# One more chunk of each FFN by seven products, its downs held back, and three smaller rearrangements

## The chip, the cores and the metric

The kernel runs on one core of a Trainium2 chip. The metric is device microseconds from launch to end. TensorE (PE) multiplies, VectorE (DVE), ScalarE (ACT) and GpSimd (POOL) do everything elementwise, and SyncE (SP) issues most transfers. Six instruction streams run beside each other and wait for one another by semaphores.

## The reference

Two layers work on 512 latent tokens and 256 context tokens of width 1024. Each layer is half an FFN, a token mixer, and half an FFN again; each of these is modulated and closed by a layer norm:

```
u = h * (1 + scale) + shift                     # from a conditioning vector: c @ w_mod
y = (silu(u @ w_in_a) * (u @ w_in_v)) @ w_out   # FFN: 1024 -> 2 x 2816 -> 1024
h = LN(ALPHA * h + 0.5 * gate * y) * g + b
```

Mixer 0 is neighbourhood attention on a 8 x 64 grid, mixer 1 grouped-query attention in a window of 128 tokens with a sink logit; both also read all context keys. In layer 1, the context is not needed after the mixer's keys and values, so the last FFN (1b) works on the 512 latent tokens alone. All is in float32.

## The kernel before, in words

Activations lie transposed: `z[d]` (128 channels x 768 tokens, d = 0 to 7) is the residual, `uh[d]` and `ul[d]` are the high and low part of the modulated input u. Every product runs as three matmuls (high x high, high x low, low x high; `mm3`, L155 to L157), so every weight is split too: `wunit` loads a unit of 128 x 2048 in four quarters (`wr`), and `split_w` makes the high part by an ACT cast (L102) and the low part by a subtraction on POOL or DVE (L104). With `mem` given, the low part is made otherwise: ACT writes the negated source (L108), and a transfer issued by POOL adds the weight to it from memory (L109, an "adding transfer"). The pairs go through a ring of 8 buffers (`RING`), the raw quarters through 5.

The four FFNs are 0a, 0b (layer 0), 1a, 1b (layer 1), all made by `ffn`. Its 2816 hidden channels are worked off in 11 chunks of 256 (`NCH`). A chunk has three units: two for a and v (`av`; `pa`, `pv`), and one for the downs (`down`; `pd`), which add gate x product to `z` (`accumulate`, L473) and so need the gate. Tokens come in two groups: a is the 512 latent and b the 256 context tokens in 0a, 0b and 1a; in 1b they are the two halves of the latent.

- Chunks 0 and 1 run plainly. In chunk 1 `sums` and `fourth` prepare combinations of u's quarters, and `fourth` overwrites half of `uh`, `ul` for d = 0 to 3; `save` has put that half to memory.
- Chunks 2 to 8 take a and v by seven products in place of eight (`seven`, after Winograd): `quarters` loads a unit's four quarters and makes seven pairs from them, three of them plain quarters (a11, a12, a22), four sums (s1 to s4). Their downs follow one unit late (`lagging`), with weights by adding transfers.
- `restore` brings the saved half back under chunk 8's downs.
- Chunks 9 and 10 run plainly: chunk 9 for group a, chunk 10 for a and then b, and chunk 9 for b with its weights loaded again (`r`).

In between lie the background products of DVE (`gemv_dve`, L202), which make later modulation vectors row by row; `tick` deals them out at a set pace. In 0a the first 33 steps (32 products) make the gate itself (`late_gate`).

A layer norm comes in parts: `sums` over d, `mean` (a matmul, L424), `centers` and squares, `variance` (L447), reciprocal root and `spreading` (L377), then `out`, which makes the next u (L305 to L310). The parts are put at named places (`plan`, `at`): the name of a down, a query tile or an attention block. `post(0)` of an FFN's end calls those of group a, `post(1)` the first of group b.

The kernel's text is a priority, not the order of an engine's queue: the framework plans each queue by a simulated time and takes what is ready. `behind(x, y)` fixes an order of two instructions of one engine. Memory comes in phases: pool "S" has 12 slabs (used for down weights, temporaries and the mixers' tiles), pool "T" the sums of u; `t2` is a set of six buffers for everybody.

Of the kernel before, what the change touches and what calls it, by code (L numbers as in the profile page):

```python
# [13 lines left out]
ALU = mybir.AluOpType  # L14
# [24 lines left out]
def hybrid_kernel(ctx: ExitStack, tc: tile.TileContext, h0, cc, crow, wmod, wmodt, bmod, lnp, wst,  # L39
# [73 lines left out]
    def phase(x):  # L113

        if phase_of[0] != x:
            phase_of[1].close()
            ph.clear()
            phase_of[0] = x
            ph[x] = phase_of[1].enter_context(tc.tile_pool(name=f"ph{x}", bufs=1, reuse_waits="tile"))

    def wunit(slabs=False, again=None, adding=False):
# [4 lines left out]
        for q in range(4):  # L126
# [3 lines left out]
            if slabs:  # L130
                hi, lo = [ph["S"].tile([P, 512], F32R, tag="slab", name=f"w{x}{nm}", bufs=SLABS) for x in "hl"]
            else:
                hi, lo = ring_pair(nm)
# [13 lines left out]
    last_pe, agenda = [None], {}  # L147
# [5 lines left out]

    def mm3(ps, a, b, first, last):
        nc.tensor.matmul(ps, a[0], b[0], start=first, stop=False)  # L155
# [131 lines left out]
    def mod_out(nm, d, c0, c1, st, prm, rm=False, dd=None):  # L287
# [12 lines left out]
        else:  # L300
            uf = ph["S"].tile([P, 512], F32, tag="slab", name=f"uf{nm}_{d}", bufs=SLABS)
# [107 lines left out]
    def layer_norm(nm, c0, c1, tag, pool=False):  # L409
# [16 lines left out]
        def centers():  # L426
            zs = [center(d, c0, c1, v["pm"]) for d in range(DT)]
# [16 lines left out]
        def variance():  # L444
            pv = bank(tag, f"pv{nm}")
            for j in range(nj):
                x = nc.tensor.matmul(pv[:, j:j + 1], v["acc"][:, j * P:(j + 1) * P], onesd[:, 0:1], start=True, stop=True)  # L447
                behind(x, prev_ln[0])
                behind(x, last_pe[0])
            ve = pv[:, 8:8 + nj]  # L450
# [3 lines left out]
        def spreading():  # L454
            v["pr"], prev_ln[0] = spread(nm, v["y"], n, tag)

# [20 lines left out]
    def ffn(nm, groups, gt, mid, post, units=(), opened={}, head=None, apart=None):  # L477

# [69 lines left out]
        def sums(j):  # L548

            x1, x2 = [bank("s", f"x{nm}_{j}_{i}")[:, 0:n2] if paced else t2(f"x{nm}_{j}_{i}")[:, 0:n2] for i in range(2)]  # L550
            x3 = t2(f"x{nm}_{j}_2")[:, 0:n2]
            k = j + 4
            op(nc.vector, x1, (uh[j], 1), (uh[j], 0), ALU.subtract)
            op(nc.vector, x1, x1, (ul[j], 1), ALU.add)
            op(nc.vector, x1, x1, (ul[j], 0), ALU.subtract)
# [3 lines left out]
            op(nc.vector, x2, (uh[k], 1), x1, ALU.subtract)  # L559
            op(nc.vector, x2, x2, (ul[k], 1), ALU.add)  # L560
# [8 lines left out]
        def fourth():  # L569

            for j in range(4):
# [5 lines left out]
                behind(nc.vector.tensor_tensor(out=x, in0=x, in1=y, op=ALU.add), evacuated[0])  # L577
# [8 lines left out]
        def quarters(u):  # L586

            src = wst[u].rearrange("p (k c) -> p k c", c=256)
            a11, a12, a21, a22 = [raw_quarter(src[:, h * 4:h * 4 + 4, m * P:m * P + P], f"{u}_{m}{h}")
                                  for m in range(2) for h in range(2)]  # L590
# [6 lines left out]
            def pair(n, src):  # L597
# [5 lines left out]
            out = [pair("a11", a11), pair("a12", a12)]  # L603
# [5 lines left out]
            return out + [pair("s4", s4), pair("s3", s3), pair("a22", a22)]  # L609
# [50 lines left out]
        late_downs, js = [], []  # L660
# [3 lines left out]
        for ci in list(range(NCH)) + [("r", NCH - 2)]:  # L664
            r = isinstance(ci, tuple)
            if not r and 0 < ci < NCH - 2:
                phase("T")
                pace[0] = each * weight[ci] / (4 if ci < s0 else 14)
                if ci == s0 - 1:
                    saved = dp.tile([2, 4, P, n2], F32, name=f"sv{nm}")  # L670
                    save(saved)
                    js = list(range(4))
                    for _ in range(1 if paced else 4):
                        sums(js.pop(0))
            if not r and s0 <= ci < NCH - 2:
# [759 lines left out]
```

## Time and profile before

| what | number |
|---|---|
| median of 3 runs (lowest to highest) | 2791.89 us (2791.28 to 2796.59) |
| the profiled execution: its time, its span | 2795.03 us, 2793.3 us |
| mean granted TensorE clock | 0.983 |
| busy: PE, DVE, POOL, ACT | 2686.0, 1819.2, 1690.1, 1214.7 us |
| matmuls | 17050 |
| read from memory, written | 312.98 MB, 12.25 MB |

The stages begin, by the trace, at about: 0a 0 us, mixer 0 575 us, 0b 1005 us, 1a 1545 us, mixer 1 2076 us, 1b 2384 us. PE's busy time has matmuls overlapping, so a busy share near one says that PE has work, not how fast it goes; the distance from one matmul to the next says that. "Busy" of a named line, its mean length and what ended the idle time before it are read from the groups of instructions; who waits for whom, from the table of waits.

### The profile page before, as it was taken

To read this page: it belongs to the slowest core of one execution; us is meant where nothing else is said; L and a number is where in the kernel's file an instruction comes from. 1 tells how busy PE (TensorE), PEld (TensorE's weight loads), DVE (VectorE), ACT (ScalarE), POOL (GpSimd) and SP (SyncE) were. 2 spreads that over 40 slices of the span, in tenths; PEclk is the share of its full clock that TensorE was granted. 3 is DMA by queue.
4 is the path that set the end of the run, shared out by engine and by line. 5 is a ranking of instruction groups with operands and counts; after the bars stand their busy time and mean duration, and the time that the engine had idled before them with its cause. 6 is when DMAs were issued, how large, how long until landed. Compare 5 with 4: busy or idle time off the path is not lost.

```text
span 2793.3 us, 48152 instructions
## 1 busy us (share of the span) xinstructions
PE 2686.0 (96%) x17050; PEld 2425.9 (87%) x17050; DVE 1819.2 (65%) x4190; ACT 1214.7 (43%) x2493; POOL 1690.1 (61%) x1528
## 2 busy tenths in 40 slices
PE   8799999999999989999999999999998999889997
PEld 5699999888888888999988899999886777889997
DVE  4977776565555686666645676666466667777744
ACT  4234343366345343443433434344246544444543
POOL 4487664474434565867644777766466446677763
PEclk9899999999999999999999999999999999999998
DMA  8465656332221213454553336467532111235562
GB/s 315 139 175 160 167 155 183 96 101 71 57 57 53 66 46 91 121 139 130 139 140 88 95 89 168 129 193 199 155 89 57 31 31 46 69 89 129 134 174 68
DMA packets 289952, 324.00 MB, mean 116 GB/s; under 512 B 28592, under 2 KB 178224, under 8 KB 288688
## 3 DMA queue, kind: packets, MB, share of 16 engines
q1 hardware_dynamic: 273296, 291.42, 35.0%
q0 software_dynamic: 16128, 29.37, 6.3%
q8 instruction: 135, 2.21, 0.3%
q14 instruction: 105, 0.86, 0.1%
q10 hardware_dynamic: 288, 0.14, 0.0%
HBM read 312.98 MB, written 12.25 MB: 116 GB/s over the span
## 4 chain that ended last, share of the span: by engine, by line
PE 80%; DVE 9%; ACT 2%; issue 2%; DMA 2%; POOL 1%; POOLq 0%; DVEq 0%; ACTq 0%; SPq 0%
PE pd0b L155 2%; PE pd1a L155 2%; PE pd0b L156 2%; PE pd0b L157 2%; PE pd1a L156 2%; PE pd1a L157 2%; PE pd0a L155 2%; PE pd0a L156 2%; PE pd0a L157 2%; DMA wr<-in_wst_dram 1%; PE wo L828 1%; PE o L828 1%; PE pd1b L155 1%; DVE z L473 1%; PE pd1b L157 1%
## 5 line engine op out<-in xcount | busy, mean ns | idle before, releaser
L104 POOL TENSOR_TENSOR wl<-wr,wh 128x512 fp32r<-128x512 f32 x296 | 389.2, 1330 | 259.8 <-ACT wh L102 192.9
L104 POOL TENSOR_TENSOR wl_s<-S,wh_s 128x512 fp32r<-128x512 f32 x210 | 279.2, 1368 | 43.3 <-ACT wh_s L102 43.1
L102 ACT CAST wh_s<-S 128x512 fp32r<-128x512 f32 x224 | 135.8, 620 | 357.0 <-POOL S L594 111.5
L102 ACT CAST wh<-wr 128x512 fp32r<-128x512 f32 x296 | 178.8, 619 | 205.1 <-DMA wr<-in_wst_dram 55.4
L202 DVE CUSTOM_DVE_ANT_0 jk<-wt,cb 128x512 f32<-128x512 f32 x364 | 247.5, 680 | 25.5 <-DMA wt<-in_wmodt_dram 21.9
L594 POOL TENSOR_TENSOR S<-wr,wr 128x512 f32<-128x512 f32 x112 | 152.9, 1365 | 157.9 <-DMA wr<-in_wst_dram 138.8
L104 POOL TENSOR_TENSOR wl_a<-wr,wh_a 128x512 fp32r<-128x512 f32 x126 | 167.6, 1383 | 14.1 <-ACT wh_a L102 11.4
L102 ACT CAST wh_a<-wr 128x512 fp32r<-128x512 f32 x168 | 103.9, 621 | 137.1 <-PE pd1b L156 19.2
L473 DVE SCALAR_TENSOR_TENSOR z<-pd0b,gt,z 128x256 f32<-128x256 f32 (+1 forms) x176 | 103.2, 602 | 57.1 <-PE pd0b L157 56.9
L473 DVE SCALAR_TENSOR_TENSOR z<-pd1a,gt,z 128x512 f32<-128x512 f32 (+1 forms) x168 | 100.0, 619 | 45.8 <-PE pd1a L157 45.3
L473 DVE SCALAR_TENSOR_TENSOR z<-pd0a,gt,z 128x512 f32<-128x512 f32 (+1 forms) x168 | 99.7, 620 | 31.3 <-PE pd0a L157 31.1
L835 POOL TENSOR_SCALAR p<-p,l 128x512 f32<-128x512 f32 x64 | 44.5, 697 | 120.8 <-DVE l L941 115.3
L323 POOL TENSOR_SCALAR z<-z,ag_None,ab_None 128x256 f32<-128x256 f32 (+1 forms) x78 | 63.2, 816 | 47.7 <-DVE uh L309 36.4
L835 POOL TENSOR_SCALAR pw<-pw,l 128x512 f32<-128x512 f32 (+1 forms) x64 | 41.2, 644 | 69.4 <-DVE l L1132 26.7
L594 POOL TENSOR_TENSOR S<-S,wr 128x512 f32<-128x512 f32 x56 | 79.9, 1428 | 4.0 <-DVE ul L579 1.4
L594 POOL TENSOR_TENSOR S<-wr,S 128x512 f32<-128x512 f32 x56 | 79.2, 1415 | 3.2 <-POOL S L594 0.4
L940 ACT ACTIVATE p<-s,m 128x512 f32<-128x512 f32 x64 | 44.0, 689 | 78.9 <-DVE m L938 73.7
L305 ACT ACTIVATE ufl<-z,bi_None,sc_None 128x256 f32<-128x256 f32 (+1 forms) x86 | 54.6, 654 | 27.4 <-DVE z L458 27.3
L473 DVE SCALAR_TENSOR_TENSOR z<-pd1b,gt,z 128x512 f32<-128x512 f32 (+1 forms) x98 | 56.6, 609 | 14.8 <-PE pd1b L157 14.5
L310 DVE TENSOR_TENSOR ul<-ufl,uh 128x256 fp32r<-128x256 f32 (+1 forms) x88 | 59.9, 686 | 3.0 <-ACT uh L307 1.6
L202 DVE CUSTOM_DVE_ANT_0 jk<-zspare,cb 128x512 f32<-128x512 f32 x84 | 57.1, 679 | 5.1 <-DMA zspare<-in_wmodt_dram 4.5
L155 PE MATMUL vn<-wh,uh 128*128 128x256 f32 x192 | 54.8, 286 | 0.9 <-DVE nq L782 0.6
(1467 smaller groups left out, 10613.5 us busy)
## 6 DMA issues: line engine op xcount, KB each, us to landing
wr<-in_wst_dram SPq DMA_DIRECT2D x520, 256.0 KB, 3.4
wt<-in_wmodt_dram SPq DMA_DIRECT2D x208, 256.0 KB, 3.9
zspare<-in_wmodt_dram SPq DMA_DIRECT2D x48, 256.0 KB, 4.4
wr_0b<-in_wst_dram SPq DMA_DIRECT2D x43, 256.0 KB, 3.2
wr_1b<-in_wst_dram SPq DMA_DIRECT2D x43, 256.0 KB, 3.2
wr_2b<-in_wst_dram SPq DMA_DIRECT2D x43, 256.0 KB, 3.4
wr_3b<-in_wst_dram SPq DMA_DIRECT2D x43, 256.0 KB, 3.5
wm<-in_wmod_dram SPq DMA_DIRECT2D x8, 1024.0 KB, 8.0
```

The lines of the kernel that those rows point to most:

```text
L102: nc.scalar.copy(hi[:], src[:])
L104: x = eng.tensor_tensor(out=lo[:], in0=src[:], in1=hi[:].bitcast(F32), op=ALU.subtract)
L155: nc.tensor.matmul(ps, a[0], b[0], start=first, stop=False)
L156: nc.tensor.matmul(ps, a[0], b[1], start=False, stop=False)
L157: last_pe[0] = nc.tensor.matmul(ps, a[1], b[0], start=False, stop=last)
L202: x = nc.vector.tensor_tensor_reduce(out=junk[:], in0=w[:], in1=cb[st], scale=1.0, scalar=0.0, op0=ALU.mult, op1=ALU.add, accum_out=out[st])
L310: return hi, nc.vector.tensor_tensor(out=lo, in0=uv, in1=uo.bitcast(F32), op=ALU.subtract)
L323: nc.gpsimd.tensor_scalar(out=zs, in0=zs, scalar1=prm[2][:, d:d + 1], scalar2=prm[3][:, d:d + 1], op0=ALU.mult, op1=ALU.add)
L473: last[0] = nc.vector.scalar_tensor_tensor(out=zt(d, c0, c1), in0=pd, scalar=gt[:, d, st:st + 1], in1=zt(d, c0, c1), op0=ALU.mult, op1=ALU ...
L594: nc.gpsimd.tensor_tensor(out=t[:], in0=a[:], in1=b[:], op=o)
L828: last_pe[0] = nc.tensor.matmul(po[64 * h:64 * h + 64, :], t[h][0], t[h][1], start=i == 0, stop=i == len(terms) - 1)
L835: nc.gpsimd.tensor_scalar(out=p, in0=p, scalar1=r, scalar2=0.0, op0=ALU.mult, op1=ALU.add)
```

## The change

1. Seven products also for chunk 9 (`for ci in range(s0, NCH - 1)`); chunk 10 alone is left plain. `restore` stands behind chunk 9's products. The end is rewritten: chunk 10's first unit for a, chunk 9's downs for a, chunk 10's second unit for a, its downs for a; then both units for b, chunk 9's downs for b and chunk 10's for b. The down weights of chunks 9 and 10 stay in a new pool "L" (16 slabs) for both groups, so nothing is loaded twice.
2. The norm of group a at this end: sums, mean and centring stand between b's units, the variance behind the second tile of chunk 10's downs for b, the spread and the rest behind the sixth. For the norms after 0a, 0b and 1a, `firm` sets PE's next matmul behind the variance's and the spread's.
3. In 0a, chunk 0's downs move into chunk 1, behind its first unit. Chunk 0 gets no background products. Two of the four `sums` there go to POOL whole.
4. In 1b, the low parts of a11, a12 and a22 are made by adding transfers instead of DVE's subtraction, and `fourth`'s addition stands behind the last accumulate.
5. In mixer 1, the centring of the last norm stands behind the last maximum of the attention, the squares behind the last exponential; the squares go to ACT with sums on POOL and DVE (`pool=False`) instead of POOL alone. Its variance and spread are each asked for one tile earlier.
6. The temporary of a 512-wide modulation lies in `t2` instead of a slab; the mixers open phase "S" themselves.

The core of the diff:

```diff
@@ mm3
-        nc.tensor.matmul(ps, a[0], b[0], start=first, stop=False)
+        behind(nc.tensor.matmul(ps, a[0], b[0], start=first, stop=False), in_front[0])
+        in_front[0] = None
...
-            uf = ph["S"].tile([P, 512], F32, tag="slab", name=f"uf{nm}_{d}", bufs=SLABS)
+            uf = t2(f"uf{nm}_{d}")
...
@@ layer_norm
+            behind(made[0], last_m[0])
...
-                nc.scalar.activation(sq, zs[d], AF.Square)
+                behind(nc.scalar.activation(sq, zs[d], AF.Square), last_m[1])
...
+            in_front[0] = x if firm else None
...
+            in_front[0] = prev_ln[0] if firm else None
...
@@ fourth
-                behind(nc.vector.tensor_tensor(out=x, in0=x, in1=y, op=ALU.add), evacuated[0])
+                behind(nc.vector.tensor_tensor(out=x, in0=x, in1=y, op=ALU.add), evacuated[0] if paced else last[0])
...
@@ quarters
-                split_w(hi, lo, src, eng=nc.vector if nb == 2 and n in ("a11", "a12", "a22", "s3") else nc.gpsimd,
-                        y=evacuated[0])
+                split_w(hi, lo, src, mem if nb == 2 else None, nc.vector if nb == 2 and n == "s3" else nc.gpsimd, evacuated[0])
...
@@ ffn
-        weight = [1.2 if bg and opened else 0] + [1.0] * (s0 - 2) + [0] + [1.0] * (NCH - 2 - s0) + [1.2]
+        weight = [0, 0] + [1.0] * (NCH - 1 - s0) + [1.5]
...
+                for _ in range(2 if opened else 1 if paced else 4):
+                    sums(js.pop(0), bool(opened))
+            w = [unit("S" if i == 2 and ci == 0 and apart else False) for i in range(1 if first_downs else 3)]
...
+            elif ci == 0:
+                avs(*[(g, i) for g in head for i in range(2)])
+                first_downs.append(dn)
             else:
+                avs((a, 0), (b, 0))
+                for f in first_downs:
+                    f(a)
+                    f(b)
+                    w += [unit(), unit()]
+                    gs += g_tiles(ci, which=(1,))
+                avs((a, 1), (b, 1))
                 dn(a)
                 dn(b)
...
+        for ci in range(s0, NCH - 1):
...
+        restore(saved)
+        phase("L")
+        u = wpos[0]
+        wpos[0] += 3
+        gl = g_tiles("l", True)
+        thin[0] = bool(bg)
+        pace[0] = each * weight[-1] / 10
+        ws = [wunit(again=u)]
+        av(ws[0], "l_0", a, *gl[0], None, 4)
+        tick()
+        wd = [wunit("L", again=u - 1)]
+        down(wd[0], f"{NCH - 2}", gs, a, True)
+        ws.append(wunit(again=u + 1))
+        av(ws[1], "l_1", a, *gl[1], None, 4)
+        tick()
...
+        wd.append(wunit("L", again=u + 2))
+        down(wd[1], "l", gl, a, True)
+        parts = post(0)
+        av(ws[0], "l_0", b, *gl[0], None, 4)
+        for f in parts[:3]:
+            f()
+        av(ws[1], "l_1", b, *gl[1], None, 4)
+        plan({f"pd{nm}_l_{b[0]}_1": parts[3:4], f"pd{nm}_l_{b[0]}_5": parts[4:]})
+        down(wd[0], f"{NCH - 2}", gs, b, True)
+        down(wd[1], "l", gl, b, True)
+        for f in post(1):
+            f()
...
@@ attn of mixer 1
+                last_m[0] = x
...
+                last_m[1] = y
...
+                at(f"wm{s}_{b}")
...
-    l4 = [ln("l4", i, g, 1, 1, 1, 6, ("mm", "o")[i], pool=i == 0) for i, g in enumerate(g1)]
+    l4 = [ln("l4", i, g, 1, 1, 1, 6, ("mm", "o")[i]) for i, g in enumerate(g1)]
...
-    plan(wo6_2=l4[0][:1], wo6_3=l4[0][1:2], wo7_2=l4[0][2:3], pow3_1_256_2=l4[0][3:4], pow3_1_256_6=l4[0][4:6],
+    plan(wo6_2=l4[0][:1], wo6_3=l4[0][1:2], wm7_3=l4[0][2:3], pow3_1_256_1=l4[0][3:4], pow3_1_256_5=l4[0][4:6],
          pow3_1_256_7=l4[1][:1])
```

More of the change, by code (lines that the diff above doesn't have):

```diff
@@ L130, in wunit @@
             if slabs:
-                hi, lo = [ph["S"].tile([P, 512], F32R, tag="slab", name=f"w{x}{nm}", bufs=SLABS) for x in "hl"]
+                hi, lo = [ph[slabs].tile([P, 512], F32R, tag="slab", name=f"w{x}{nm}", bufs={"S": SLABS, "L": 16}[slabs])
+                          for x in "hl"]
             else:
@@ L608, in quarters @@
             s3 = tt(3, a11, a21, ALU.subtract)
-            return out + [pair("s4", s4), pair("s3", s3), pair("a22", a22)]
+            return out + [pair("s4", s4), pair("s3", s3), pair("a22", a22, mems[3])]
         def seven(un, u, gh, gl):
@@ L742, in ffn @@
+            if ci == 0 and apart:
                 for g in head:
```

182 lines of the change are left out of this document (79 added, 103 removed).

## The prediction

> **What bounds the kernel now.** I read the page's busy times and chain first, then the table of waits of TensorE (PE), then windows of time around each place that the change touches.
>
> ```profile
> span 2793.3 us, 48152 instructions
> PE 2686.0 (96%) x17050; PEld 2425.9 (87%) x17050; DVE 1819.2 (65%) x4190; ACT 1214.7 (43%) x2493; POOL 1690.1 (61%) x1528
> PE 80%; DVE 9%; ACT 2%; issue 2%; DMA 2%; POOL 1%; POOLq 0%; DVEq 0%; ACTq 0%; SPq 0%
> ```
>
> PE is busy 96% of the span and carries 80% of the chain. So the time is PE's work plus PE's few idle places. Here are the waits that matter (total, times, longest, in us):
>
> ```profile
> PE pd0a L155 <- DVE z L473: 14.3, 2, 14.0
> PE pd1b L155 <- DVE z L473: 4.5, 3, 2.7
> PE pd1b L155 <- DVE gl1b L624: 4.4, 3, 1.7
> PE pow L156 <- DVE wol L832: 2.2, 1, 2.2
> ```
>
> One hole of 14.0 us stands at the downs of chunk 0 in 0a. In 1b, PE waits for late DVE work for 8.9 us. At the end of mixer 1, it waits 2.2 us.
>
> How fast PE goes, by window (length, PE busy with matmuls, PEld, DVE, ACT, POOL, granted clock, DMA share, GB/s):
>
> ```profile
> 473.73:495.52 21.79, 21.79 (x99) 18.02 (x97) 3.08 (x7) 6.80 (x12) 10.45 (x9) 1.00 0.36 110
> 112.15:117.90 5.75, 5.75 (x50) 5.75 (x48) 5.48 (x13) 3.24 (x6) 4.49 (x5) 1.00 0.31 95
> 442.47:457.08 14.61, 14.61 (x86) 14.61 (x85) 9.41 (x24) 8.51 (x16) 8.08 (x8) 1.00 0.95 236
> 2440.81:2452.33 11.52, 11.52 (x99) 11.52 (x97) 11.52 (x19) 3.98 (x11) 8.88 (x9) 1.00 0.31 89
> 2546.82:2566.85 20.03, 20.03 (x170) 20.02 (x168) 15.05 (x26) 12.32 (x25) 12.54 (x11) 1.00 0.55 134
> ```
>
> The windows' edges add a few instructions to the counts. Row 1 holds the 96 matmuls of 512 columns of one chunk's a and v (0.227 us each); row 2 holds 48 of 256 columns (0.120). Row 3 is one unit by seven products, 84 matmuls of 384 columns (0.174). Rows 4 and 5 are 1b: half a chunk plainly, and a whole chunk by seven products (168 matmuls, 1.43 us a product).
>
> **The change part by part.** The sum is made against the profiled execution, 2795.0 us (span 2793.3 and 1.7 around it). That is 3.1 above the median of the runs, 2791.9.
>
> *Chunk 9 by seven products.* Plainly it costs 21.79 + 2 x 5.75 = 33.3 us of PE in 0a, 0b, 1a, and 2 x 11.52 = 23.0 in 1b. By seven products it is 2 x 14.61 = 29.2 and 20.0. The downs stay the same. That is -4.1 three times and -3.0: **-15.3 us**. Rows 3 and 5 show PE full with the other engines below it, so one more such chunk stays PE's. Chunk 9's second load and split of its first two units goes, which relieves POOL.
>
> *Chunk 0 of 0a.* The hole, the stretch after it, and the rows around it:
>
> ```profile
> 75.90:89.90 14.00, 0.05 (x1) 0.00 (x0) 13.27 (x41) 0.21 (x1) 0.00 (x0) 0.61 0.71 224
> 89.95:95.98 6.03, 6.03 (x16) 4.86 (x17) 5.54 (x11) 0.00 (x0) 0.00 (x0) 0.50 0.16 46
> 88.42 0.17 DVE L275 TENSOR_SCALAR gt<-mod 128x16 f32<-128x16 f32 x1
> 66.05 5.06 POOL L104 TENSOR_TENSOR wl<-wr,wh 128x512 fp32r<-128x512 f32 x4 [3.63 <-PE pv0a L156]
> L499 DVE TENSOR_TENSOR pv0a<-pv0a,sl0a x13: 417/700/700, 58.5 to 551.1; 128x512 f32<-128x512 f32 x8, 128x256 f32<-128x256 f32 x5
> ```
>
> PE fills six PSUM banks, then waits until DVE has made the gate (gt) from 33 products; after that its clock is 0.50 for 6.03 us, which wastes 3.0. Together that is 17.0. In the new order, the first unit of chunk 1 (16.6 us, half of 33.3) comes first. Its weights are split by 66.05 + 5.06 = 71.1, quarter by quarter as PE takes them, so it runs from 67.4 to 84.0. Six downs (48 x 0.227 = 10.9 for eight, so 8.2) carry PE to 92.2. The evacuation of that unit puts two operations a group more on DVE, of the last row's length: 2 x 0.70 + 2 x 0.42 = 2.2 us. So the gate comes at 90.6, before 92.2. No hole is left. The second unit's weights need ring slots that the deferred downs free only at their end (about 101). POOL then also has 16 operations of the sums, which used to be DVE's. I put 2 us of PE on that: **-15** (bounds -17 and -5, the latter if the split queues behind most of the sums).
>
> *The norm of group a at the ends of 0a, 0b, 1a.* The last down of a, the mean, the last sum of squares, the variance, the spread, the first use, the last u; then, of later places, a wait, a first use and a window:
>
> ```profile
> 545.10 0.39 PE L157 MATMUL pd0a<-gh0a,wl 128*128 128x512 f32 x1
> 550.84 1.02 PE L424 MATMUL pml<-asl,onesd 128*128 128x512 f32 x2
> 562.60 0.68 DVE L335 TENSOR_TENSOR aql<-ppl,sql 128x512 f32<-128x512 f32 x1
> 566.12 0.95 PE L447 MATMUL pvl<-onesd,aql 128*128 128x1 f32 x8
> 570.45 1.05 PE L377 MATMUL prl<-idn,yl 128*128 128x128 f32 x8
> 574.79 0.40 PE L155 MATMUL pq<-uh,wh 128*128 128x512 f32 x1
> 588.44 0.76 DVE L310 TENSOR_TENSOR ul<-ufl,uh 128x512 fp32r<-128x512 f32 x1
> PE pa1b L155 <- DVE uh L309: 3.3, 2, 2.1
> 2079.37 0.39 PE L157 MATMUL vw<-wh,ul 128*128 128x256 f32 x1 [0.85 <-DVE ul L310]
> 2384.00:2389.60 5.60, 5.60 (x27) 5.60 (x28) 5.60 (x17) 5.04 (x11) 4.07 (x7) 0.50 0.15 46
> ```
>
> Count from the end of a's downs, 545.3 (one matmul after 545.10). Variance is at +20.8, spread at +25.1, first use at +29.5. Before, 34.5 us of b's work (288 matmuls x 0.120) cover that; now, since chunk 9's a and v are done for b too, it is 192 x 0.120 = 23.0. The new places put the mean after 5.75 us of b, as before, and the variance at d = 1, about +20 with mean and variance themselves (sum of squares ready at +18). Spread is asked for at d = 5 (+23.5) but the reciprocal root takes from 566.12 + 0.95 to 570.45 = 3.4 us, so about +24.3. Being firm, PE stands there for 0.8; two downs later (+26.8) it waits for u, ready 4.3 after the spread, +28.6. That is 2.6 each for 0a and 0b. In 1a, PE takes the eight rows of u faster than they come: 8 x 4 blocks x 3 x 0.120 = 11.5 us against 588.44 + 0.76 - 574.79 = 14.4. Before, 34.5 - 25.1 = 9 us of b's work were left to fill in after the spread, now two downs are. So 2.6 + 2.9, less the 0.85 that it waits already: 5. **+10** (0 if b's engines are quicker, 20 if DVE is full).
>
> A hole also lowers the clock: the last row above is 0.50 for 5.6 us, right behind pa1b's wait of 2.1. The Trainium skill, "TensorE: Matmul & The Clock Gate", section "What's actually happening", lets the clock fall after an idle window of about 3.4 us; by that rule none of these holes would cost clock and the sum would be 3.4 lower. The trace halves it sooner, so I count two stretches of 3.4 us at half speed, **+3.4** (0 to 7).
>
> *Restoring u.* Before, it lies under chunk 8's downs. Now the a and v of chunk 10 follow at once.
>
> ```profile
> 455.00 0.33 SPq L94 DMA_DIRECT2D wr<-in_wst_dram  x1
> 455.52 0.60 SPq L584 DMA_DIRECT2D ul<-sv0a  x1
> 460.15 0.61 SPq L584 DMA_DIRECT2D ul<-sv0a  x1
> DMA to landing us min/median/max: 4.7/4.8/4.8
> ```
>
> Eight transfers are issued on SP from 455.52 to 460.15, landing 4.7 later: the last at 464.9, 7.8 after the seven products end at 457.08. PE starts with k = 4 to 7: 12 x 0.227 = 2.7 us for a, 5.5 with v. If v's half goes ahead, 0.3 is lost, in order 3.0; in 1b (matmuls half as long) 2.5 to 5. I take 0.7 three times and 3: **+5** (3 to 14). The first row shows a weight load that the text puts behind the restore going out ahead of it: the order is a planner's, so I don't queue the loads behind it.
>
> *1b's plain quarters.* Three of the seven pairs per unit lose DVE's subtraction and get an ACT copy and an adding transfer on POOL.
>
> ```profile
> 2534.00:2598.00 64.00, 62.87 (x436) 58.32 (x436) 46.37 (x77) 31.43 (x66) 46.11 (x36) 1.00 0.54 133
> L104 DVE TENSOR_TENSOR wl_a<-wr,wh_a 128x512 fp32r<-128x512 f32 x13 | 13.1, 1020 | 1.8 <-ACT wh_a L102 1.8
> L108 ACT ACTIVATE wl_0b<-wr_0b 128x512 fp32r<-128x512 f32 x2 | 1.3, 627 | 0.0
> L109 POOL DMA_DIRECT2D wl_1b<-in_wst_dram x7: 865/865/866, 2496.5 to 2678.2; - x7
> DMA to landing us min/median/max: 5.2/6.9/8.5
> q0 software_dynamic: 1158, 2.11, 19.4%
> L594 POOL TENSOR_TENSOR S<-wr,wr 128x512 f32<-128x512 f32 x112 | 152.9, 1365 | 157.9 <-DMA wr<-in_wst_dram 138.8
> ```
>
> In 64 us (two chunks) DVE drops by 12 x 1.02 to 34.1, ACT rises by 12 x 0.63 to 39.0, POOL by 12 x 0.87 to 56.5, and the DMA share by 12/8 of 19.4% to 0.83. DVE's lateness (8.9 us) should halve, the fourth sums now placed behind the last accumulate helping: **-4** (-9 to +20; the bad end is a rival below).
>
> *Mixer 1's norm.*
>
> ```profile
> 2361.20 2.40 DVE L351 TENSOR_TENSOR z<-z,pml 128x256 f32<-128x256 f32 x7
> 2363.52 0.68 DVE L1108 TENSOR_REDUCE m<-sw 128x1 f32<-128x512 f32 x1
> ```
>
> The last maximum stands behind the centring for 2.4 us. Exchanged, the 2.2 us wait goes, perhaps one half-clock stretch too (1.7). The squares leave POOL for ACT, the variance is asked for one tile earlier; the norm itself starts later and may take part back: **-3.5** (-5 to +3).
>
> Paces of the background products change by under one product a chunk, except some six more in the last chunk of 0a beside a full DVE; `t2` instead of slabs for one temporary: nothing, with the bounds of the norm's term.
>
> Sum: -15.3 - 15 + 10 + 3.4 + 5 - 4 - 3.5 = **-19.4**, so 2775.6 for the profiled execution and 2772.5 on the median's scale.
>
> **The rivals.** *Ends without holes*: if the planner hides norm and restore, +18.4 goes and the time is 2754. For it: variance and spread ask within 1 us of readiness. Against: the cover shrinks by 11.5 us.
>
> *The ends give it all back*: norm 20, restore 14, clock 7 instead of 18.4 is -19.4 + 22.6 = +3, time 2795; nearly the same if the wait in 0a merely moves. For it: firm places make PE stand.
>
> *Adding transfers come late in 1b* (slower). A pair's slot is free seven products before its use: 7 x 1.43 = 10.0 us. Two ACT operations (0.63 each) and a landing of 6.9 take 8.2; a POOL operation of 1.37 ahead of it leaves 0.4. With 0.83 of the DMA engines taken, landings may grow. Where two units stand with no downs between, once a chunk, PE would wait. Eight chunks at 4 us each, instead of the 4 gained, is -15.4 + 32: 2808. It decides (beyond no change) from 15.4/8 = 1.9 us per chunk. The Trainium skill, "DMA: Bandwidth & Descriptors", section "Anatomy of one DMA — SWDGE (gpsimd) path", fits 2.0 us + bytes / 436e3 per transfer, by which 256 KB would land in an estimated 2.6 us and this rival would have no chance; the trace's 6.9 says otherwise and decides.
>
> *Loads behind the restore* (slower): if SP kept the text's order, PE would wait some 9 us at four ends, 36 and more: 2803.
>
> **How the numbers follow.** Forecast 0.66, no holes 0.13, given back 0.10, late transfers 0.07, loads behind 0.04. 0.2% (5.6 us) is about what a measurement of this kernel can tell from no change: faster 0.79, same 0.10, slower 0.11. The range, 2754 to 2790, reaches from the case without holes nearly to the one that gives all back, and leaves out 0.2.
>
> **What would show it.** Right: chunk 9 as 168 shorter matmuls; no 14 us hole near 76; holes of 1 to 3 us before the first matmuls of mixer 0, 1a, mixer 1 and of chunk 10; fewer DVE waits in 1b. Wrong: PE in 1b waiting for wl_a landings, SP loads behind the restore, or a new hole near 101 for chunk 1's weights.

## The result, and the profile after

The changed kernel takes 2821.49 us (median of 4 runs, 2819.34 to 2824.49), the kernel before 2791.59 in the same sitting: ratio 1.0101, 95% interval 1.0088 to 1.0113. It is 1.0% slower, where 0.7% faster was forecast.

The page of the changed kernel (span; busy time, share of the span and instructions of each engine):

```profile
span 2821.6 us, 48014 instructions
PE 2685.3 (95%) x16954; PEld 2432.2 (86%) x16954; DVE 1815.5 (64%) x4201; ACT 1228.0 (44%) x2533; POOL 1737.9 (62%) x1573
```

96 matmuls are gone, PE's busy time is all but the same, and the span is 28 us longer: waits came. The table of PE's waits (who waits, for whom, total us, times, longest):

```profile
PE p61b L166 <- DMA wl_a<-in_wst_dram: 22.0, 10, 4.2
...
PE p21b L163 <- DVE ul L595: 5.7, 1, 5.7
PE pd0a L163 <- DVE T0a_3l L580: 4.8, 1, 4.8
...
PE pd0a L163 <- DVE gl0a L639: 3.7, 1, 3.7
...
PE p01b L166 <- DMA wl_a<-in_wst_dram: 3.1, 4, 1.1
```

Of before's rows, the 14.0 us hole at pd0a has shrunk, and 1b's waits for DVE are smaller. New are 25.1 us, in these two rows, for the landing of plain quarters' low parts (`wl_a`) in 1b, 5.7 for `fourth` (L595) in 1b, and one wait of 3.7 in the seventh chunk of seven products of 0a. By stages (distance in us between first matmuls, the profiled executions; the fastest kernel found below beside them; 0b's first matmul in before stands at 998.6):

| stage | before | after | e18 |
|---|---|---|---|
| start to chunk 2 of 0a | 152.2 | 146.4 | 146.8 |
| chunk 2 to mixer 0 | 422.6 | 430.9 | 424.5 |
| mixer 0 | 423.8 | 423.9 | 421.7 |
| 0b | 546.9 | 547.6 | 545.2 |
| 1a | 531.1 | 528.3 | 530.4 |
| mixer 1 | 307.4 | 303.8 | 302.4 |
| 1b | 409.4 | 440.5 | 398.4 |

1b alone lost 31 us. What it looks like there, first before, then after, over the same 120 us (length, busy of PE, PEld, DVE, ACT and POOL, granted clock, share of the 16 DMA engines, GB/s; then the DMA queues: packets, MB, share):

```profile
2520.00:2640.00 120.00, 118.86 (x822) 110.42 (x821) 86.57 (x146) 59.62 (x123) 86.97 (x69) 1.00 0.56 137
q1 hardware_dynamic: 18396, 12.07, 35.2%
q0 software_dynamic: 2304, 4.20, 20.5%
```

```profile
2520.00:2640.00 120.00, 108.59 (x714) 99.12 (x713) 56.94 (x105) 61.18 (x123) 97.21 (x80) 0.97 0.83 158
q0 software_dynamic: 12129, 8.31, 50.1%
q1 hardware_dynamic: 16128, 10.49, 32.8%
```

VectorE was relieved as meant (86.6 to 56.9), and PE got 714 matmuls done instead of 822. The adding transfers (q0) take 50.1 / 8.31 = 6.0% of the DMA engines' time per MB (rows of 512 B and of 2 KB together), plain loads (q1) 3.1%; so bytes rose by 15%, the engines' busy share from 0.56 to 0.83.

One stall, in the POOL queue and in the chain of waits of the changed kernel:

```profile
2540.92 1.30 POOL L109 DMA_DIRECT2D wl_a<-in_wst_dram  x1 [2.72 <-PE p21b L165]
2541.72 1.42 POOL L109 DMA_DIRECT2D wl_0b<-in_wst_dram  x1
2542.27 1.76 POOL L109 DMA_DIRECT2D wl_1b<-in_wst_dram  x1
2543.13 1.79 POOL L109 DMA_DIRECT2D wl_2b<-in_wst_dram  x1
2544.41 1.39 POOL L109 DMA_DIRECT2D wl_3b<-in_wst_dram  x1
2545.21 1.92 POOL L109 DMA_DIRECT2D wl_a<-in_wst_dram  x1
```

```profile
2540.92 7.81 DMA wl_a<-in_wst_dram
2548.86 0.36 PE p61b L166
```

Six adding transfers leave within 4.3 us: a22 of one unit, the four quarters of the lagging down unit, and the next plain quarter. The first lands 7.81 later, and PE has stood for 2.93 of it. That landing is only part of the delay. By the ring of 8 (eight pairs back in the program's order), this a22 takes the buffers that the product p51b of the unit before has read:

```profile
2534.02 0.28 PE L166 MATMUL p51b<-T1b_3h,wl_s 128*128 128x256 f32 x1
2539.81 0.63 ACT L108 ACTIVATE wl_a<-wr 128x512 fp32r<-128x512 f32 x1
```

They are free at 2534.30; ACT writes the negated copy at 2539.81, POOL issues at 2540.92, 6.6 us after they were free, and PE wants the pair at 2545.93 (2548.86 - 2.93), 11.6 after. Six of the ten waits at p61b, 17.6 of the 22.0 us, are of this kind: the transfer is the first of six, is issued 3.4 to 5.6 us before PE needs it and lands 7.4 to 7.9 after its issue.

### The profile page after: what moved, and what is told of

It is laid out like the page before. It is cut to its first block, busy times and chain, and to the rows that moved or that the text cites. A ratio compares the mean times of both kernels' runs of the same rounds, so it can differ in the third digit from the quotient of the medians.

```text
span 2821.6 us, 48014 instructions
## 1 busy us (share of the span) xinstructions
PE 2685.3 (95%) x16954; PEld 2432.2 (86%) x16954; DVE 1815.5 (64%) x4201; ACT 1228.0 (44%) x2533; POOL 1737.9 (62%) x1573
## 5 line engine op out<-in xcount | busy, mean ns | idle before, releaser
L104 POOL TENSOR_TENSOR wl<-wr,wh 128x512 fp32r<-128x512 f32 x200 | 261.5, 1325 | 148.7 <-ACT wh L102 91.6
L104 POOL TENSOR_TENSOR wl_s<-S,wh_s 128x512 fp32r<-128x512 f32 x240 | 314.1, 1344 | 57.0 <-ACT wh_s L102 56.6
L102 ACT CAST wh_s<-S 128x512 fp32r<-128x512 f32 x256 | 155.7, 621 | 404.9 <-POOL S L610 114.4
L610 POOL TENSOR_TENSOR S<-wr,wr 128x512 f32<-128x512 f32 x128 | 173.3, 1354 | 172.7 <-DMA wr<-in_wst_dram 171.1
L104 POOL TENSOR_TENSOR wl_a<-wr,wh_a 128x512 fp32r<-128x512 f32 x144 | 189.6, 1364 | 22.6 <-ACT wh_a L102 14.4
L102 ACT CAST wh_a<-wr 128x512 fp32r<-128x512 f32 x192 | 118.6, 620 | 135.8 <-issue 23.0
L102 ACT CAST wh<-wr 128x512 fp32r<-128x512 f32 x200 | 120.6, 617 | 95.2 <-DMA wr<-in_wst_dram 17.7
L610 POOL TENSOR_TENSOR S<-S,wr 128x512 f32<-128x512 f32 x64 | 101.1, 1579 | 1.7
L610 POOL TENSOR_TENSOR S<-wr,S 128x512 f32<-128x512 f32 x64 | 87.8, 1371 | 3.4
L109 POOL DMA_DIRECT2D wl_a<-in_wst_dram x48 | 69.8, 1588 | 15.6 <-ACT wl_a L108 5.2
```

Source lines behind the costliest of these rows:

```text
L102: nc.scalar.copy(hi[:], src[:])
L104: x = eng.tensor_tensor(out=lo[:], in0=src[:], in1=hi[:].bitcast(F32), op=ALU.subtract)
L109: nc.gpsimd.dma_start(flat_or_tiles(lo, mem), mem, accum_op=ALU.add)
L610: nc.gpsimd.tensor_tensor(out=t[:], in0=a[:], in1=b[:], op=o)
```

## The experiments

Before ran beside each batch (medians 2793.1 to 2795.4), so ratios to it are compared; 0.10% is 2.8 us. Each ratio's interval is 0.1 to 0.28% to either side, so two runs whose ratios differ by 0.1% are not told apart.

| run | what | median us | ratio to before (95%) |
|---|---|---|---|
| e1 | after, adding transfers of 1b undone | 2798.59 | 1.0013 (1.0002 to 1.0023) |
| e2 | before, with them | 2815.27 | 1.0082 (1.0065 to 1.0100) |
| e3 | after, a22 undone | 2822.87 | 1.0104 (1.0089 to 1.0119) |
| e4 | after, rows of 2 KB | 2809.02 | 1.0054 (1.0035 to 1.0073) |
| e5 | e1, `fourth` early | 2791.22 | 0.9983 (0.9972 to 0.9995) |
| e6 | e1, sums behind the downs | 2798.70 | 1.0014 (1.0003 to 1.0025) |
| e7 | e1, derive of 0a's norm late | 2796.61 | 1.0006 (0.9994 to 1.0017) |
| e8 | e1, not firm | 2791.60 | 0.9991 (0.9980 to 1.0001) |
| e9 | e5, derive of mixer 0's norm late | 2786.75 | 0.9972 (0.9961 to 0.9983) |
| e10 | e9, not firm | 2777.82 | 0.9951 (0.9934 to 0.9969) |
| e11 | e5, chunk 0's downs in place | 2803.23 | 1.0033 (1.0022 to 1.0045) |
| e12 | e10 and e6 | 2784.09 | 0.9961 (0.9948 to 0.9973) |
| e13 | e10, adding transfers back | 2802.22 | 1.0030 (1.0018 to 1.0043) |
| e14 | e13, rows of 2 KB | 2792.08 | 0.9992 (0.9979 to 1.0006) |
| e15 | e14, POOL relieved | 2805.22 | 1.0045 (1.0028 to 1.0062) |
| e16 | e13, POOL relieved | 2817.27 | 1.0081 (1.0064 to 1.0097) |
| e17 | e13, down units by POOL | 2775.38 | 0.9937 (0.9916 to 0.9959) |
| e18 | e14, down units by POOL | 2772.99 | 0.9930 (0.9902 to 0.9958) |

### The adding transfers of 1b

e1 undoes this part in the changed kernel, e2 does it alone in the kernel before:

```diff
-split_w(hi, lo, src, mem if nb == 2 else None, nc.vector if nb == 2 and n == "s3" else nc.gpsimd, evacuated[0])
+split_w(hi, lo, src, None, nc.vector if nb == 2 and n in ("a11", "a12", "a22", "s3") else nc.gpsimd, evacuated[0])
```

> The changed kernel with its part 4 taken back in one place: in 1b the low parts of a11, a12 and a22 are DVE's subtraction again, all else stays. Theory T1 (the adding transfers of these quarters land after PE needs them: 26.3 us of PE waits for wl_a in 1b, and six half-clock stretches of 3.4 us more than before, about 10): 2821.5 falls by 30 to 40, to 2782 - 2792, and the waits for wl_a from a transfer are gone. Rival T2 (1b is slower because of its eighth chunk by seven products and the new end, and the transfers only show it): it stays above 2810. In both, the hole at the gate of 0a and the one at 425 us stay.

> The kernel before with the adding transfers of a11, a12 and a22 in 1b alone. T1: seven chunks instead of eight wait, so 2791.6 rises by 7/8 of 30 to 40, less the 4.4 us of waits for gl1b that DVE no longer causes: 2814 - 2822. T2: within 5 us of 2791.6, or faster.

The part costs 0.88% taken out (25 us, less than the 30 to 40 of the theory and far from its rival) and 0.82% put in alone (23 us, as forecast). e3 puts only a22 back on VectorE (`mem if nb == 2 and n != "a22"`), since PE waits at p61b, a22's product:

> The changed kernel, with a22 alone back on DVE; a11 and a12 keep their adding transfers. 22.0 of the 26.3 us of waits are those of the seventh product (a22), 4.3 those of the first and second. If each pair is late for itself: 2821.5 falls by 22 and most of the clock's 10, to 2789 - 2799, with 3 to 6 us of waits for wl_a left. If a queue of transfers is late as a whole (POOL's or the DMA engines'), the waits move to the first two products and it falls by under 12, staying above 2809.

Nothing is won; the waits move to the plain quarters that are left (15.5 + 6.2 us against 22.0 + 3.1):

```profile
PE p01b L166 <- DMA wl_a<-in_wst_dram: 15.5, 6, 3.9
PE p11b L166 <- DMA wl_a<-in_wst_dram: 6.2, 4, 4.2
```

So it is not a22's place alone. e4 stores 1b's weights so that a quarter's row in each partition is one piece of 2 KB instead of four of 512 B:

```diff
-src[:, h * 4:h * 4 + 4, m * P:m * P + P]
+src[:, h * 4:h * 4 + 4, m * P:m * P + P] if nb == 3 else wst[u, :, (m * 2 + h) * 512:(m * 2 + h + 1) * 512]
```

> The changed kernel with the weights of 1b's chunks 2 to 9 laid out by quarters, so that a quarter is one row of 2 KB per partition and not four of 512 B; the adding transfers stay. On POOL they are issued in 1.30 us in place of 0.87 for the down weights, which have 2 KB rows, and they bring 25,300 more packets. If the short rows make them late: the median landing in 1b falls from 7.7 to about 6.9, issues to 0.87, and 15 to 30 of T1's loss comes back (2792 - 2806). If the landing itself is too long for the ring whatever the rows: it falls by 2 to 10 (2811 - 2819) and the waits for wl_a stay over 18.

That recovers 0.47% of the 0.88, 12 to 13 us, between the two expectations. The issue on POOL (min/median/max ns), after and e4:

```profile
L109 POOL DMA_DIRECT2D wl_a<-in_wst_dram x42: 1252/1298/3085, 2476.1 to 2711.4; - x42
```

```profile
L109 POOL DMA_DIRECT2D wl_a<-in_wst_dram x45: 856/898/1802, 2474.5 to 2720.0; - x45
```

With four times the pieces the median issue takes 1.30 us instead of 0.90. For the other half, e13 to e16 put the part on the best kernel by then (e10), with long and short rows, and with the low parts of s1, s2 and s4 moved from POOL to VectorE (`n[0] == "s"` for `n == "s3"`), so that POOL has three operations fewer per unit:

> The fastest kernel so far (e10) with the change's adding transfers for a11, a12 and a22 in 1b put back, rows of 512 B. Theory (they alone cost 20 to 23 us, as e2 and e1 say): 2777.8 + 20 to 23 = 2798 to 2801, with waits of TensorE for wl_a of 15 us or more in 1b. Rival (much of their price was fourth's late place, which e5 mended): 2777.8 + 12 at most.

> e13 with the plain quarters of 1b laid out so that each partition's row is 2 KB in one piece. Theory A (the length of the pieces is what makes the transfers late): at most 4 us above e10, 2778 to 2782. Theory B (half is the pieces, the other half the queue of GpSimd, in which six adding transfers per chunk wait behind its two-input operations; e4 won back 12.4 of 23 us): 2786 to 2790.

> e14 with the low parts of s1, s2 and s4 in 1b taken by VectorE instead of GpSimd (VectorE then has as many weight operations as in e10, GpSimd three fewer per unit). Theory B: the rest of the loss goes, 2777 to 2781. Theory A': the transfers land too late whatever GpSimd does, since the ring gives them only 10 us: within 2 us of e14.

> e13 with the low parts of s1, s2 and s4 in 1b taken by VectorE, rows of 512 B as in the change. Theory B: GpSimd issues the transfers 1.3 to 3 us sooner, half of e13's loss goes, 2786 to 2791. Theory A: the pieces of 512 B keep them late, at most 4 us below e13, 2794 or more.

e13 costs 0.79% again, whatever `fourth` does. e14 recovers 0.38. In e15 and e16 POOL is freer, and the time is longer by 0.5%; e15 in the window used above:

```profile
2520.00:2640.00 120.00, 105.10 (x676) 96.52 (x675) 72.36 (x121) 60.89 (x120) 64.51 (x60) 0.96 0.72 156
```

```profile
PE p01b L166 <- DMA wl_a<-in_wst_dram: 20.7, 5, 4.5
```

POOL is down to 64.5 us of 120 and PE does fewer matmuls still; the waits stand at a11's product now. So POOL's work ahead of the transfers is not what holds them up: that theory falls. In e15, POOL itself stands before these issues and waits for ACT's copies (from 2475 to 2720; the changed kernel has 4.4 us in this row):

```profile
POOL wl_a L109 <- ACT wl_a L108: 28.6, 10, 4.1
```

(Why this version is slower than e14 stays open otherwise: it also changes VectorE's order.) e17 and e18 leave each disputed transfer as it is and take the lagging down unit's four off the queue:

```diff
-w = wunit(again=u, adding=True)
+w = wunit(again=u, adding=nb == 3)
```

> e13 (adding transfers for a11, a12, a22 in 1b) with the low parts of 1b's lagging down units taken by GpSimd's subtraction instead of adding transfers: six adding transfers a chunk instead of ten. Theory (the loss is the share of the 16 DMA engines: adding transfers moved 8.3 MB in 120 us of 1b and took 50.1% of the engines' time, plain loads 10.5 MB for 32.8%, 0.83 in all, and everything lands late): the share falls to about 0.65, the waits for wl_a to a third, total 2784 to 2793 instead of 2802.2. Rival (each transfer with pieces of 512 B is late by itself, or GpSimd's queue holds it; GpSimd then has 4 x 1.3 us in place of 4 x 0.87 to 2 us a chunk): within 4 us of 2802, or above.

> The same with rows of 2 KB in one piece. Theory: the share of the adding transfers falls further (4.9% of the engines' time per MB instead of 6.0%), total 2778 to 2784, as good as e10. Rival: within 4 us of e14's 2792.1.

That gives 0.93% back with short rows, 0.62% with long ones: better than forecast, and these two have the lowest medians here (their intervals overlap with e10's). The landing times of `wl_a` (us from issue) in e13, e14, e17 and e18, then the window in e17 and in e18:

```profile
DMA to landing us min/median/max: 4.5/6.5/12.8
```

```profile
DMA to landing us min/median/max: 4.2/5.7/10.6
```

```profile
DMA to landing us min/median/max: 4.4/5.7/6.9
```

```profile
DMA to landing us min/median/max: 4.1/5.9/6.9
```

```profile
2520.00:2640.00 120.00, 119.04 (x817) 110.28 (x816) 65.00 (x125) 62.18 (x129) 119.04 (x92) 1.00 0.78 151
```

```profile
2520.00:2640.00 120.00, 120.00 (x829) 111.65 (x828) 67.69 (x126) 63.45 (x132) 110.22 (x93) 1.00 0.66 153
```

The theory of those two runs was only half right. The share of the DMA engines fell to 0.78 in e17, not 0.65; the median landing fell by 0.8 there and rose by 0.2 in e18; POOL is now busy for 119 of 120 us in e17, and its issues are no faster. The late end of the landings went, 12.8 to 6.9, but those were the last of the six, which PE needs only behind the downs. The long waits are for the first of the six, and for it two things changed at once. It now lands 5.1 to 5.7 us after its issue in e17 (7.4 to 7.9 in the changed kernel). And the framework planned PE's queue anew. From the end of the unit's third product to its seventh, with the matmuls of the downs alone (length; busy and count of PE, PEld and DVE), in the changed kernel and in e17:

```profile
2540.72:2548.86 8.14, 1.89 (x6) 0.92 (x6) 0.00 (x0) 1.00 0.90 170
```

```profile
2516.30:2526.25 9.95, 6.40 (x26) 4.70 (x26) 2.51 (x4) 1.00 0.76 168
```

26 of the 48 matmuls of the downs now stand ahead of p61b, 6 did before: some 4.7 us of work (20 of 0.234), in which the transfer may land; it is issued 7.0 to 7.8 us before PE needs it. Either change would have taken most of the wait: a landing of 7.4 to 7.9 against 7.0 to 7.8, or one of 5.1 to 5.7 against 3.4 to 5.6. No run holds PE's order and takes the four transfers away, so what the queue is worth by itself is not shown. What is shown is that with the down units off the queue the plan as a whole no longer waits. Whether the long landings come from the order within the queue or from the DMA engines' load in those microseconds, these runs do not tell.

### `fourth` in 1b

```diff
-behind(nc.vector.tensor_tensor(out=x, in0=x, in1=y, op=ALU.add), evacuated[0] if paced else last[0])
+behind(nc.vector.tensor_tensor(out=x, in0=x, in1=y, op=ALU.add), evacuated[0])
```

> The changed kernel with the low parts of a11, a12 and a22 in 1b back on VectorE (e1), and in 1b the fourth operand built behind the last gl of chunk 1 again, as before the change, and not behind its last accumulate. Theory (in e1 the first product that reads a T tile waits 5.7 us for ul, and 6.8 us of half clock follow): the 5.97 us gap at 2463.29 and its half clock go, the eight chunks of seven products take 265.2 - 6 to 8 = 257 to 259 us, total about 2791. Rival (the chain of 12 VectorE operations only moves between the accumulates and delays a bank of the downs): the time stays within 2 us of e1's 2798.6.

0.30% less than e1, 8 us, the total that was forecast. The stretch was not: the wait of 5.7 at p21b is gone, but the eight chunks by seven products take 242.8 us instead of 265.2 (257 to 259 expected), their first matmul coming 5.9 later (e1's profile is of its longest run, e5's of one of its shortest, and e1's also has 6.1 us more of waits of pd1b for gl1b). So the part costs 8 us by the runs, and how these divide is open, since the two profiles differ by more there than the runs do. What the profiles show is that the wait went: with the additions behind the last accumulate, PE had nothing to do between the second and the third product.

### The start of 0a

> e1 with the last two sums of 0a taken after the deferred downs of chunk 0 instead of between the two groups of chunk 1. Theory (the gate comes at 101.5 and not at 90.6 because two sums and their T splits stand between the 33 gate products on VectorE): the gate comes at 88 to 94, the 5.15 us hole at 90.5 and the half clock at 93.5 to 107 go, chunk 2 starts at 136 to 140 instead of 145.0, total about 2791. Rival (the 33 gate products themselves set the gate, since their 33 weight tiles load no sooner): the gate stays after 99 and the time within 2 us of e1's. Second rival (the sums come late for the first product that reads a T tile): a wait of p20a on a T tile of 3 us or more takes the place of the hole.

> e5 with the downs of chunk 0 in 0a back in chunk 0, ahead of chunk 1; two of the four sums stay on GpSimd. Theory (deferring the downs was worth 7.3 us, counted from VectorE's first background product to the third chunk of seven products: 152.5 before, 145.2 after): that stretch takes 152 to 154 us again instead of 145.2, total 2797 to 2800. Rival (VectorE, busy without a break from the gate to chunk 2, is the bound, so that the place of the downs matters little): the stretch takes 147 or less and the time stays within 2 us of e5's 2791.2.

e6 takes the last two sums behind the deferred downs (on e1), e11 runs chunk 0's downs in chunk 0 (on e5):

```diff
-if ci == s0 - 1 and js:
+if ci == s0 - 1 and js and (not opened or i == 1):
```

```diff
-first_downs.append(dn)
+dn(a)
+dn(b)
```

The gate in the changed kernel, in e6 and in e11:

```profile
101.54 0.31 DVE L284 TENSOR_SCALAR gt<-mod 128x16 f32<-128x16 f32 x1
```

```profile
94.02 0.30 DVE L284 TENSOR_SCALAR gt<-mod 128x16 f32<-128x16 f32 x1
```

```profile
89.09 0.30 DVE L284 TENSOR_SCALAR gt<-mod 128x16 f32<-128x16 f32 x1
```

Executions start up to 4 us apart, so count from VectorE's first background product (61.7, 60.6 and 60.6): the gate comes 39.8, 33.4 and 28.5 later, 27.7 in before (60.7). The second unit of chunk 3 (the "third chunk" of e11's expectation) starts 145.2, 142.6 and 151.4 later, 152.5 in before. So deferring the downs is worth 6 to 7 us of that stretch, and e6's gate, 6 us sooner, only 2.6 more; its time is e1's, as the rival had it. Why the rest is given back is open: VectorE is not busy throughout (in e6 8.3, 9.1, 8.3, 3.6, 9.8 and 9.6 us of each 10 from 80 to 140). By the kernel's time e11 says more than by the stretch: it is 12 us longer than e5 (0.50%, 14 us, by the ratios), past its forecast of 2797 to 2800. Its stages 0b and 1b, which the edit does not touch, are 4.4 and 3.9 us longer in the profiles; this too is open.

### The small operation that took 8 us

The wait of 3.7 us for `gl0a` has this above it, in VectorE and POOL of the changed kernel:

```profile
419.33 7.96 DVE L273 TENSOR_TENSOR bi_None<-sc_None,lnp_sb 128x16 f32<-128x16 f32 x1
```

```profile
418.25 1.58 POOL L610 TENSOR_TENSOR S<-S,wr 128x512 f32<-128x512 f32 x1
419.51 2.81 POOL L104 TENSOR_TENSOR wl_a<-wr,wh_a 128x512 fp32r<-128x512 f32 x2
422.02 1.55 POOL L610 TENSOR_TENSOR S<-wr,S 128x512 f32<-128x512 f32 x1
423.28 1.53 POOL L610 TENSOR_TENSOR S<-wr,wr 128x512 f32<-128x512 f32 x1
424.53 2.72 POOL L104 TENSOR_TENSOR wl_s<-S,wh_s 128x512 fp32r<-128x512 f32 x2
```

An operation on 16 elements per partition, 0.17 us elsewhere, ends with POOL's last operation of an unbroken series, 427.29 against 427.25.

> e1 with the six small operations that derive the scale and the bias of 0a's norm ordered on VectorE behind the accumulates of group a at the end of 0a (some 100 us later), out of chunk 8's products. Theory (one 128x16 operation held VectorE for 8.99 us while six two-input operations ran on GpSimd without a break, and TensorE lost 4.1 us and ran at half clock for 6.8 us behind it): no VectorE operation over 3 us is left at 410 to 430, the gap goes, 0a's stage from chunk 2 to mixer 0 shortens from 431.7 by 5 to 8 us, total about 2792. Rival (whatever VectorE operation falls there is held as long, the stream on GpSimd being the cause and not this operation): another operation of VectorE is held for 4 us or more, and the time stays within 2 us of e1's 2798.6.

> The last kernel with the fourth operand early (e5), and the six small operations that derive scale and bias of mixer 0's norm, which stood on VectorE in the seventh chunk of seven products of 0a, ordered behind the accumulates of group a's last downs. (e7 moved the derive of another norm, one that falls elsewhere, and so did not try this.) Theory (a small VectorE operation whose operands all lie in SBUF is held for as long as GpSimd's two-input operations follow one another without a break, 9 us here, and TensorE loses 5.2 us to it and runs at half clock for 6.8 us): the chunk that took 38.7 us from one p00a to the next but one takes 31.2 to 32.5, 0a from chunk 2 to mixer 0 shortens from 433.4 to 425 to 428, total 2784 to 2787. Rival (as in e6, the operation that then falls there, the sum of the background products, is held in its place): the chunk stays at 37 us or more and the time within 2 us of e5's 2791.2. Second rival (the operation is held for as long at its new place, at the end of 0a): the loss moves to the end of 0a and the time stays.

> e10 with the last two sums of 0a behind the deferred downs (as in e6). Theory (e6's start of 0a was 2.4 us shorter than e1's, no more, since VectorE has the same operations to do): 2 to 3 us less than e10, total 2778 to 2782. Rival (e6's time was no shorter than e1's, since the stretch is given back): within 1 us of e10.

```diff
@@ derive(..., y=None): its first operation behind(..., y); before ffn("0a", ...)
+plan(pa0a_l_0_512=[lambda: cur.update(l1=derive(0, 1, 0, 6, y=last[0]))])
```

That is e9; e7 had `l0=derive(0, 0, 0, 3, y=last[0])`, the derive of another norm. It left these six operations where they were, and there the next of them (L274) was held for 8.93 us. From chunk 8's first unit to its second, with chunk 7's downs between, in e5 and in e9:

```profile
400.70:439.40 38.70, 33.88 (x183) 30.99 (x182) 34.44 (x64) 11.79 (x22) 20.73 (x18) 0.91 0.51 130
```

```profile
401.10:432.40 31.30, 31.30 (x183) 29.32 (x182) 25.93 (x60) 11.68 (x22) 20.02 (x18) 1.00 0.61 153
```

7.4 us are back in the trace, the half clock behind the hole included; 0.11% (3 us) by the ratios, which is within their intervals. In e9, no VectorE operation takes over 3 us any more. In e6 and e12 (in this order), with the last two sums elsewhere, another operation stood in the same place and was held instead:

```profile
413.82 9.54 DVE L243 TENSOR_TENSOR mod<-ga,bmod_sb 128x64 f32<-128x64 f32 x1
```

```profile
414.99 8.96 DVE L284 TENSOR_SCALAR gt<-mod 128x16 f32<-128x16 f32 x2
```

It is the place beside POOL's series, not the operation: four different ones were held there. e12, forecast 2 to 3 us below e10, came out 6 above it by the medians and 3 by the ratios, within their intervals; PE's wait for `gl0a` is back in it, 5.7 us.

### The firm places

> e1 with the products of the variance and of the spread of group a's norm at the ends of 0a, 0b and 1a not put ahead of the products that follow in the program (the edges of order that the change added are left out). Theory (TensorE waits at these places because the order makes it): the holes of 3.7, 3.5 and 4.6 us at the three ends go, but the order of the program puts variance and spread behind the whole of group b's downs, so that mixer 0, 0b's chunk 0 and mixer 1 wait for the norm instead: total 2 to 12 us longer than e1's 2798.6. Rival (ends without holes): the norm is early enough without the places, total 2789 to 2795.

> e9 without the edges of order that put variance and spread of group a's norm ahead of the products that follow at the ends of 0a, 0b and 1a. Theory after e8 (the places cost mixer 1 3.3 us and the ends nothing): 3 us less than e9, all of it in mixer 1 (304.2 to 301), total 2781 to 2784. Rival (e8's 7 us against e1 came from the norms' places at all three ends): 6 us or more less than e9.

```diff
-l0 = [ln("l0", i, g, 0, 0, 0, 3, "o", firm=i == 0) for i, g in enumerate(g2)]
+l0 = [ln("l0", i, g, 0, 0, 0, 3, "o") for i, g in enumerate(g2)]
```

Without these edges (l2 and l3 alike) the kernel is 0.22% and 0.21% faster, 6 us each time: e8's theory, that they help, falls, and so does e10's, that mixer 1 alone pays for them. The profiles do not say where: the waits before the spread and the first use stay (2.4 + 1.8 us at the end of 0a in e10), mixer 1 is 3.3 and 1.4 shorter, and the rest lies in stages that differ by as much between runs of one order. Left open.

## Why the prediction was wrong, step by step

The step that failed first of all is the term of 1b's plain quarters: it let their adding transfers land in time. Step by step, in the order of the sum:

- *Seven products for chunk 9*, -15.3: as forecast where it can be read. A unit takes 14.6 to 14.7 us in 0a and, where nothing waits (e10), 10.0 in 1b; no run takes this part out alone.
- *Chunk 0 of 0a*, -15, within its bounds: -7.3 by the stretch (-6.2 by e11's), -12 to -14 by e11's time, of which the rest is not explained. What failed is "So the gate comes at 90.6": it came at 101.5. The step priced the evacuation on VectorE (2.2 us) and not the two sums and the T splits (L552, L580) that also went between the gate's products; with those two sums elsewhere (e6) the gate comes 6.4 us sooner. The hole came back at 90.9 as 4.8 us.
- *The norm at the ends*, +10: PE's waits for the norm are 4.1 us behind 0a, 3.2 behind 0b and 6.8 behind 1a, against 0, 0 and 3.3 before, so 10.8 more. Variance, spread and first use in 0a stand at 569.6, 574.0 and 577.3 from T0 = 547.5: +22.1, +26.5, +29.8 for the forecast +20, +24.3, +28.6. That making them firm costs some 6 us on top (0.21% and 0.22%) was not seen.
- *The clock behind these holes*, +3.4: in the changed kernel, no stretch of half clock starts within 25 us behind the ends of 0a and 0b, and the one at 2093.7 belongs to the same product (vw) as before's at 2085.9. Over-priced by 3.4, inside its bounds (0 to 7).
- *Restore*, +5: 0.3 us in 0a (e1) and 0.2 to 0.7 in 1a and 1b (e1, e5, e10) of waits for the restored half; the changed kernel's profile shows none. Over-priced by 4 or more.
- *1b's plain quarters*, -4, measured +23 to +25: the step that failed. "Two ACT operations (0.63 each) and a landing of 6.9 take 8.2; a POOL operation of 1.37 ahead of it leaves 0.4" mis-sized both parts. From the free buffer to the issue it had 2.6 us; the stall shown above has 6.6. The landing of 6.9 was a median over transfers of a queue that held only the four of a down unit; the ones that PE stood for took 7.4 to 7.9. The share of 0.83 came out as forecast, but no term of the sum was drawn from it. The rival of late transfers named this mechanism, priced it at 4 us a chunk (it was about 3), and got 0.07. The 2.6 us estimate that the prediction works out from the Trainium skill's formula ("DMA: Bandwidth & Descriptors", "Anatomy of one DMA — SWDGE (gpsimd) path") stands against 4.3 to 12.4 measured here for adding transfers.
- *"the fourth sums now placed behind the last accumulate helping"*: wrong sign, +8 (e5).
- *"Paces of the background products change by under one product a chunk ... nothing"*: wrong. The new paces moved the derive from 373 to 419 us, into POOL's series: 7.4 us in the trace, 3 by the ratios of e5 and e9.
- *Mixer 1's norm*, -3.5: the stage goes from 307.35 to 303.84, and the 2.2 us wait is gone. The agreement to 0.1 is luck: the same stage also holds the waits behind 1a, 3.5 us more than before, and is 3.3 and 1.4 shorter without the firm places.

Put together, by runs that undo one part after the other: the adding transfers 0.88% (25 us, e1), the late `fourth` 0.30% (8, e5), the held operation 0.11% (3, e9, not clear of noise), the firm places 0.21% (6, e10). That is 1.50%, 42 of the 49 us between 2821.5 and the forecast 2772.5. e10 is left at 0.9951 of before, where the forecast was 0.9931; of the 6 us left, the 4 that the plain quarters were to gain are the largest named part; chunk 0, the clock and the restore have no run of their own that would settle theirs.

## What to carry to other kernels

A transfer with a deadline is priced from the moment its buffer is free: first the way through the queues of the engines that prepare and issue it (6.6 us in the stall above, 2.6 in the forecast), then its landing in the bunch in which it is issued (7.4 to 7.9), not the median of an emptier queue (6.9). List what the same queues do in those microseconds. And when an edit moves a transfer, look whether the plan also moved the product that waits for it. When the pace of background work changes, find out beside what its rare small steps will fall. And where an operation is ordered behind another "to help", write down which product waits for it and what else PE has until then.

## What the hardware showed

- Per MB, adding transfers take 6.9% of 120 us of the 16 DMA engines in rows of 512 B (e17, 43.1 / 6.29) and 4.9 to 5.0% in rows of 2 KB (before, 20.5 / 4.20; e18, 31.3 / 6.28); a plain load takes about 3%. The median issue of 256 KB takes POOL 1.30 us with rows of 512 B and 0.90 with rows of 2 KB. The adding transfers' queue in e17, then in e18, over the 120 us used above (packets, MB, share):

```profile
q0 software_dynamic: 12672, 6.29, 43.1%
```

```profile
q0 software_dynamic: 3451, 6.28, 31.3%
```

- Four small VectorE operations (L273, L274, L243, L284) were held for 8 to 9.5 us while POOL ran operations with two inputs without a break. The Trainium skill, "SBUF — State Buffer", section "SBUF: two separate sides", says that the port pair which the two engines share goes to the one that starts first for the whole instruction, and the other is blocked (of VectorE's operations, those with two inputs in SBUF or in a two-port mode). The traces agree on the blocking; but here six POOL instructions in a row went ahead of the one that waited.
- In 1b, PE's clock is 0.5 for 27.3 us in the changed kernel, 6.8 in before and 3.4 in e18, in stretches of 3.4 and 6.8 us (the first and the last microseconds of 1b left out). In the changed kernel such stretches begin at 2513.6, 2622.8, 2660.3 and 2694.5, during or within 1.5 us behind waits of 4.2, 2.7, 3.2 and 2.1 us; at waits of 2.9 (2548.9) and 2.5 us (2729.3) none begins, so here the length of the wait alone does not decide.
